# A hybrid encoder layer: the weight sums of the block products move to GpSimd, and the last 256 columns get a bank of their own

## The chip, the cores and the metric

The kernel runs on one core of a Trainium2 chip. TensorE (PE) multiplies matrices and accumulates in PSUM banks; VectorE (DVE) and ScalarE (ACT) work element by element on SBUF and PSUM; GpSimd (POOL) does so on SBUF; SyncE (SP) issues most transfers. The metric is the time of one execution on the device, in microseconds (us); less is better.

## The reference

One layer of an encoder for 512 tokens of width 1024 in float32: a pre-norm, an input projection, two token mixers in parallel (a gated linear recurrence, and a gated delta rule in chunks of 64), an output projection, then the feed-forward part, which is all that the change touches:

```python
h = rmsnorm(x, ffn_norm[l])
gu = h @ w_gate_up[l]                     # 512 x 1024 by 1024 x 5632
gt, up = jnp.split(gu, 2, axis=-1)
x = x + (jax.nn.silu(gt) * up) @ w_down[l]  # 512 x 2816 by 2816 x 1024
...
return rmsnorm(x, final_norm)
```

## The kernel before

**Splitting.** Every fp32 operand of a large matmul is split into two parts that PE takes at its faster rate: ACT copies the tile into a rounded type (`hi`), DVE subtracts to get the rest (`lo`), and three products hi·hi, hi·lo, lo·hi are accumulated. `parts_of` (L1258) does this for one tile: a copy on ACT, and a subtraction on DVE that reads two tiles in SBUF.

**Block products.** The feed-forward part cuts each product of matrices into 2 x 2 blocks and forms it from seven products in place of eight (the scheme of Strassen and Winograd). This needs sums and differences of blocks of both operands ahead of PE, and folds of the banks behind it.

- `gate_up` (L1320) makes one tile of 128 hidden columns. The first two of the 22 tiles are made plainly; the other 20 run through `gate_up`. SP loads two weight tiles `rg`, `ru` of 128 x 1024 (tag `wraw`, three buffers for all). The four sums `t1` to `t4_` (128 x 512) of their quarters b11, b12, b21, b22 are made, then all is split, and seven products of 12 matmuls of 256 columns each, 84 in all, follow. Five DVE instructions read the banks.
- The down projection contracts over 11 pairs of hidden tiles (`n2_` = 11). `down_first(j)` (L1408) uses weight block b11 and the three sums b11+b12, b12+b22 and b11+b12+b22 for four products into eight banks A, B, C, D (two each), 24 matmuls of 512 columns. DVE then folds the banks into the output `x1` and its halves. `down_second(j)` (L1432) uses the second row of blocks and one sum `t4_` for three more products, 18 matmuls; the last three j (`LASTK` = 3) are held back and end the kernel, one output block of 128 tokens after another (`last_mm`, L1516), each followed by its final norm (`finish_half`, `finish`, `write`).
- `t2_`, the sum of all three blocks, is kept in the buffers `hh` and `hl` of the normed input (`keep2`), since `down_second` needs it again; those buffers are free only when the last product of `gate_up` is done.
- `down_sums(j)` (L1114) makes two of the three sums of `down_first` in advance. It runs during the first eleven `gate_up` blocks: SP loads the blocks into `bg` and `bgb`, DVE makes two sums of 128 x 512, and SP writes them to the DRAM tile `sums`. `down_first` loads them from there.

**What sets the order.** Each helper only records its operations (class `Rec`). `Plan.order` (L148) then plays all of them through with its own costs and due times, and emits a fixed order for each engine; a due time is that of the stage (`TIMES`) plus the offset `plan.t`, and an operation can't be taken before its tiles have free buffers. So all instructions have the same line in the profile, L375, and are told apart by their tiles. In an engine's queue an instruction that waits holds up all behind it.

**At the end** the last 512 columns of token block 1 are made as twice 256 columns in the same bank of D: nine matmuls, a DVE instruction that adds the bank's first 256 columns to `x1`, nine matmuls, a DVE instruction for the second 256.

Of the kernel before, what the change touches and what calls it, by code (L numbers as in the profile page):

```python
# [26 lines left out]
NF = D_FF // P  # L27
# [20 lines left out]
N2, N4, NW = 14, 22, 3  # L48
AHEAD = 12.0
# [331 lines left out]
def trunk(ctx: ExitStack, tc: tile.TileContext, x, mix_norm, w_in, rg_conv_w, rg_conv_b, rg_wa, rg_ba, rg_wx, rg_bx,  # L381
# [3 lines left out]
    plan = Plan(nc)  # L385
    V, A, G, T = Rec(plan, "DVE", nc.vector), Rec(plan, "ACT", nc.scalar), Rec(plan, "POOL", nc.gpsimd), Rec(plan, "PE", nc.tensor)
    Q = Rec(plan, "SP", nc.sync)
# [3 lines left out]
    wp = ctx.enter_context(tc.tile_pool(name="wp", bufs=2))  # L391
# [2 lines left out]
    dn = ctx.enter_context(tc.tile_pool(name="dn", bufs=1))  # L394
    hp = ctx.enter_context(tc.tile_pool(name="hp", bufs=1))
    sp = ctx.enter_context(tc.tile_pool(name="sp", bufs=2))
    dr = ctx.enter_context(tc.tile_pool(name="dr", bufs=1, space=DRAM))
    ps = ctx.enter_context(tc.tile_pool(name="ps", bufs=3, space=PSUM))

    uid = [0]  # L400
# [5 lines left out]
    def new(pool, shape, tag, bufs, dt=F32):  # L406
        return plan.tile(pool, shape, dt, tag, bufs, nm(tag))
# [10 lines left out]
    def two(dt=F32, shape=(P, 512)):  # L418
        return new(t2, shape, "t2", N2, dt)
# [687 lines left out]
    rg_flush()  # L1107
    for n in range(KD):
        rnn_part(1, n)

    wdn = w_down[0].rearrange("(j h p) n -> p j h n", p=P, h=2)
    sums = {}

    def down_sums(j, after):  # L1114

        now = plan.t
        r, b22 = new(wp, (P, 2, 512), "bg", 2), new(wp, (P, 512), "bgb", 2)
        plan.extra = after
        Q.dma_start(r, wdn[:, j, 0, :].rearrange("p (h n) -> p h n", h=2))
        Q.dma_start(b22, wdn[:, j, 1, 512:D])  # L1120
        plan.extra = ()
        V.tensor_tensor(r[:, 0, :], r[:, 0, :], r[:, 1, :], ALU.add)
        V.tensor_tensor(r[:, 1, :], r[:, 1, :], b22, ALU.add)
        sums[j] = new(dr, (P, 2, 512), "sums", NF // 2)
        Q.dma_start(sums[j], r)
        plan.t = now

    gates = [(rnn_gate, n) for n in range(KD)] + [(dn_gate, n) for n in range(KD)]
    for g in range(4):
        spend()  # L1130
# [24 lines left out]
    for n in range(KD):  # L1155
# [1 line left out]
        y = four(F32R)  # L1157
        split(mixs[n // 2][:, n % 2, :], y)
        mh.append(y)
    last_split = (len(plan.ops) - 1,)  # L1160
    spend()


# [94 lines left out]
    def parts_of(src, hi, lo, ahead):  # L1258
        now = plan.t
        plan.t = now - ahead  # L1260
        A.copy(hi, src)
        V.tensor_tensor(lo, src, f(hi), ALU.subtract)
        plan.t = now
# [56 lines left out]
    def gate_up(n):  # L1320
        spend(10.2)
        now = plan.t
        rg, ru = new(wp, (P, 8, P), "wraw", NW), new(wp, (P, 8, P), "wraw", NW)
        plan.t = now - 40
        Q.dma_start(rg, wg[:, :, n * P:(n + 1) * P])
        Q.dma_start(ru, wg[:, :, D_FF + n * P:D_FF + (n + 1) * P])
        b11, b21, b12, b22 = rg[:, 0:4, :], rg[:, 4:8, :], ru[:, 0:4, :], ru[:, 4:8, :]
        t1, t2_, t3, t4_ = (two(shape=(P, 4, P)) for _ in range(4))
        plan.t = now - 24
        for t, x_, y_ in ((t1, b11, b12), (t2_, t1, b22), (t3, b12, b22), (t4_, t2_, b21)):  # L1330
            V.tensor_tensor(t, x_, y_, ALU.add)
        plan.t = now
        gh_, gl_ = new(wp, (P, 8, P), "whi", 2, F32R), new(wp, (P, 8, P), "wlo", 2, F32R)
        parts_of(rg, gh_, gl_, AHEAD)
        w7 = {"1": (gh_[:, 0:4, :], gl_[:, 0:4, :]), "2": (gh_[:, 4:8, :], gl_[:, 4:8, :])}
        ah, al = new(wp, (P, 8, P), "whi", 2, F32R), new(wp, (P, 8, P), "wlo", 2, F32R)
        bh, bl = four(F32R, (P, 8, P)), four(F32R, (P, 8, P))
        for i, (name, src, hi, lo) in enumerate((("6", t2_, ah, al), ("7", t3, ah, al), ("5", t1, bh, bl), ("4", t4_, bh, bl))):
            j = 4 * (i % 2)
            w7[name] = hi[:, j:j + 4, :], lo[:, j:j + 4, :]  # L1340
            parts_of(src, *w7[name], AHEAD - 1.4 * i)
        w7["3"] = two(F32R, (P, 4, P)), two(F32R, (P, 4, P))
        parts_of(b22, *w7["3"], AHEAD - 7)
# [12 lines left out]
        V.tensor_tensor(u[:, hi_], m, pc, ALU.subtract)
        product(pa, w7["2"], xs7["2"], False)
        act(s_[:, lo_], pa, AF.Silu)
        product(pd_, w7["5"], xs7["5"], True)
        V.tensor_tensor(u[:, hi_], pd_, u[:, hi_], ALU.add)  # L1360
        product(pc, w7["4"], xs7["4"], False)
        V.tensor_tensor(s_[:, hi_], pc, m, ALU.subtract)
        act(s_[:, hi_], s_[:, hi_], AF.Silu)
        product(pd_, w7["3"], xs7["3"], False)
        V.tensor_tensor(u[:, lo_], pd_, m, ALU.add)
        V.tensor_tensor(fa[n // 2][:, n % 2, :], s_, u, ALU.mult)

    for n in range(BRIDGE, NF):
        if n - BRIDGE < NF // 2:
            down_sums(n - BRIDGE, last_split)  # L1370
        gate_up(n)


# [34 lines left out]
    def down_first(j):  # L1408

        spend(5.5)  # L1410
        now = plan.t
        r1, r2 = new(wp, (P, 2, 512), "wraw", NW), new(wp, (P, 2, 512), "wraw", NW)
        hi, lo = new(wp, (P, 2, 512), "whi", 2, F32R), new(wp, (P, 2, 512), "wlo", 2, F32R)
        t2_ = keep2[j // 8][:, j % 8, :]
        plan.t = now - 40
        Q.dma_start(r2, sums[j])
        Q.dma_start(r1[:, 0, :], wdn[:, j, 0, 0:512])
        Q.dma_start(r1[:, 1, :], wdn[:, j, 1, 512:D])
        plan.t = now - 16
        V.tensor_tensor(t2_, r2[:, 0, :], r1[:, 1, :], ALU.add)  # L1420
        plan.t = now
        parts_of(r1[:, 0, :], hi[:, 0, :], lo[:, 0, :], AHEAD)
        parts_of(t2_, hi[:, 1, :], lo[:, 1, :], AHEAD)
        hi2, lo2 = four(F32R), four(F32R)
        parts_of(r2, hi2, lo2, AHEAD)
        x4 = down_q(j, True)
        w4 = [(h[:, i, :], l[:, i, :]) for h, l, i in ((hi, lo, 0), (hi, lo, 1), (hi2, lo2, 1), (hi2, lo2, 0))]
        for bank, w, x_ in zip("ABCD", w4, x4):
            for i in range(2):
                down_mm(banks[bank][i], i, w, x_, j == 0, j == n2_ - 1)  # L1430

    def down_second(j):  # L1432

        now = plan.t
        r = new(wp, (P, 2, 512), "wraw", NW)
        hi, lo = four(F32R), four(F32R)
        plan.t = now - 40
        Q.dma_start(r, wdn[:, j, 1, :].rearrange("p (h n) -> p h n", h=2))
        t4_ = two()
        plan.t = now - 16  # L1440
        V.tensor_tensor(t4_, keep2[j // 8][:, j % 8, :], r[:, 0, :], ALU.add)
        plan.t = now
        parts_of(r, hi, lo, AHEAD)
        th, tl = two(F32R), two(F32R)
        parts_of(t4_, th, tl, AHEAD)
        x3 = down_q(j, False)
        return {"2": ((hi[:, 0, :], lo[:, 0, :]), x3[2]), "3": ((hi[:, 1, :], lo[:, 1, :]), x3[0]), "4": ((th, tl), x3[1])}
# [65 lines left out]
            V.scalar_tensor_tensor(xv, xv, rin, gain3[:, n0:n0 + 256], ALU.mult, ALU.mult)  # L1513
            Q.dma_start(out[0, c * P:(c + 1) * P, n0:n0 + 256], xv)

    def last_mm(name, i, po, n0=0, n=512):  # L1516
        spend(0.7 * LASTK * n / 512)
        for w3 in last:
            (wh, wl), x_ = w3[name]
            down_mm(po[:, n0:n0 + n], i, (wh[:, n0:n0 + n], wl[:, n0:n0 + n]), x_, False, w3 is last[-1], True)  # L1520

    def weighted(c):
        xg = two()
        V.tensor_tensor(xg, x1[c][:, 0:512], gain3[:, 0:512], ALU.mult)
        return xg

    for i in range(2):
# [3 lines left out]
    for i in range(2):  # L1531
        last_mm("2", i, banks["A"][i])
        finish_half(i, 0, banks["A"][i])
        xg = weighted(i)
        if i == 0:
            last_mm("3", i, banks["D"][i])
            finish_half(i, 1, banks["D"][i])
        else:
            for n0 in (0, 256):
                last_mm("3", i, banks["D"][i], n0, 256)  # L1540
                xv = x1[i][:, 512 + n0:768 + n0]
                V.tensor_tensor(xv, banks["D"][i][:, n0:n0 + 256], xv, ALU.add)
                A.activation(two()[:, 0:256], xv, AF.Square, accum_out=ssf[:, i, 1 + n0 // 256:2 + n0 // 256])
        write(i, xg, finish(i))
    with tc.manual_schedule():
        todo = plan.order()
# [30 lines left out]
```

## Time and profile before

| | us |
|---|---|
| time, median of 3 runs | 1084.93 (1083.03 to 1085.01) |
| the profiled execution's own time | 1083.75 |
| its span in the trace | 1082.0 |
| the plain tiles and `gate_up`, on PE | up to about 963 |
| `down_first` and `down_second`, on PE | about 963 to 1064 |
| the last products and the final norm | 1064 to 1082 |

The span runs from the first to the last instruction of the trace; the rest of the time lies around it. A group of the profile names engine, operation and tiles (out<-in, without buffer numbers; many scratch tiles are just `t`), its count, busy time and mean duration. A timeline row has the start and duration in us, and in brackets how long the engine was idle before it and what ended that. `ax`, `mm` and `st` are PSUM tiles, `na` holds `x1`. Where instructions on one engine overlap, the start-to-start distance is less than the duration.

### The profile page before, as it was taken

The numbers are of one execution on the slowest core, as the hardware profiler recorded it, in microseconds if no ns is written. First come the engines' busy times: TensorE is split into PE (matmuls) and PEld (weight loads), VectorE is DVE, ScalarE is ACT, GpSimd is POOL, SyncE is SP. The second block draws the span as 40 slices with busy tenths as digits, with TensorE's granted clock in tenths as the row PEclk, the third lists the DMA queues.
The fourth block names the chain that finished last, engine by engine and source line by source line (L and its number), as shares of the span: only waits on it lengthen the run. The fifth ranks groups of instructions, "written<-read, shape, count | busy, mean of one in ns | idle before, by whom it ended". The sixth has DMA issues, their size and how long they took to land.

```text
span 1082.0 us, 17706 instructions
## 1 busy us (share of the span) xinstructions
PE 1053.9 (97%) x6793; PEld 918.9 (85%) x6793; DVE 903.2 (83%) x1631; ACT 654.8 (61%) x1182; POOL 44.2 (4%) x93
## 2 busy tenths in 40 slices
PE   6999999999999999999999999999999999999996
PEld 6988788887888888788798878689999999998885
DVE  6677999779895898689748856869999999889997
ACT  6868898887348653756566254337454454456754
POOL 2000000002020100030001000000000000000000
PEclk9999999999999999999999999999999999999998
DMA  7333323232331034103311323395475434436632
GB/s 196 97 95 100 98 64 88 83 93 73 96 90 55 25 108 116 42 20 102 93 36 45 87 75 108 109 302 159 143 228 180 128 97 114 117 101 210 196 118 96
DMA packets 165893, 118.59 MB, mean 110 GB/s; under 512 B 5681, under 2 KB 152225, under 8 KB 165809
## 3 DMA queue, kind: packets, MB, share of 16 engines
q1 hardware_dynamic: 164336, 114.18, 35.5%
q10 hardware_dynamic: 1184, 3.15, 0.8%
q8 instruction: 53, 0.87, 0.3%
q14 instruction: 32, 0.25, 0.1%
q0 software_dynamic: 288, 0.13, 0.1%
HBM read 109.59 MB, written 7.86 MB: 109 GB/s over the span
## 4 chain that ended last, share of the span: by engine, by line
PE 82%; DVE 4%; ACT 2%; issue 0%; DVEq 0%; ACTq 0%
PE mm L375 48%; PE ax L375 21%; PE st L375 13%; DVE t L375 3%; ACT na L375 1%; ACT t L375 1%; DVE na L375 1%; DVE wlo L375 0%; ACT ax L375 0%; ACT whi L375 0%; ACT L375 0%; DVEq L1572 0%; ACT drt L375 0%; DVE rin L375 0%; ACT rst L375 0%
## 5 line engine op out<-in xcount | busy, mean ns | idle before, releaser
L375 DVE TENSOR_TENSOR t<-t,t 128x512 fp32r<-128x512 f32 (+15 forms) x466 | 245.9, 540 | 14.6 <-ACT t L375 8.6
L375 PE MATMUL mm<-hh,whi 128*128 128x512 f32 (+2 forms) x704 | 242.7, 356 | 1.1 <-ACT whi L375 1.1
L375 PE MATMUL mm<-hl,whi 128*128 128x512 f32 (+2 forms) x704 | 242.2, 355 | 0.0
L375 ACT CAST whi<-wraw 128x1024 fp32r<-128x1024 f32 (+3 forms) x142 | 133.4, 940 | 152.5 <-PE mm L375 109.0
L375 DVE TENSOR_TENSOR wlo<-wraw,whi 128x1024 fp32r<-128x1024 f32 (+3 forms) x141 | 153.5, 1090 | 71.2 <-ACT whi L375 31.2
L375 PE MATMUL mm<-hh,wlo 128*128 128x512 f32 (+1 forms) x688 | 154.4, 355 | 1.1 <-DVE wlo L375 1.1
L375 PEld LDWEIGHTS mm<-hh,whi 128*128 128x128 f32 (+1 forms) x704 | 132.3, 188 | 18.8 <-ACT whi L375 1.9
L375 PEld LDWEIGHTS mm<-hl,whi 128*128 128x128 f32 (+1 forms) x704 | 132.4, 188 | 17.1 <-DVE hl L375 0.2
L375 PE MATMUL ax<-t,t 32*32 32x32 f32 (+3 forms) x1071 | 142.3, 286 | 4.0 <-DVE na L375 3.8
L375 PEld LDWEIGHTS mm<-hh,wlo 128*128 128x128 f32 x688 | 116.1, 189 | 18.6 <-DVE wlo L375 1.5
L375 PEld LDWEIGHTS ax<-t,t 128*128 128x128 f32 (+1 forms) x1071 | 111.3, 160 | 18.9 <-DVE na L375 4.0
L375 ACT CAST t<-t 128x512 fp32r<-128x512 f32 (+1 forms) x128 | 82.0, 651 | 31.5 <-DVE t L375 29.0
L375 PE MATMUL mm<-t,t 128*128 128x256 f32 (+1 forms) x468 | 91.2, 336 | 0.0
L375 PE MATMUL mm<-t,whi 128*128 128x512 f32 x320 | 82.0, 398 | 2.6 <-ACT t L375 1.8
L375 DVE SCALAR_TENSOR_TENSOR t<-mm,par,t 128x511 f32<-128x511 f32 (+1 forms) x108 | 79.9, 743 | 3.7 <-ACT t L375 2.9
L375 PEld LDWEIGHTS mm<-t,t 128*128 128x128 f32 x468 | 72.9, 190 | 8.9 <-DVE t L375 0.2
L375 ACT ACT_TABLE_LOAD x58 | 74.4, 1283 | 5.8 <-PEq L1563 1.7
L375 ACT ACTIVATE t<-t 128x128 f32<-128x128 f32 (+4 forms) x84 | 45.8, 558 | 50.3 <-DVE t L375 47.0
L375 PEld LDWEIGHTS mm<-t,whi 128*128 128x128 f32 x320 | 60.0, 190 | 17.1 <-ACT t L375 2.4
L375 ACT CAST t<-wraw 128x1024 fp32r<-128x1024 f32 (+1 forms) x48 | 41.8, 872 | 33.3 <-DMA wraw<-in_w_gate_up_dram 19.2
L375 DVE TENSOR_TENSOR t<-wraw,t 128x1024 fp32r<-128x1024 f32 (+1 forms) x48 | 47.9, 1000 | 1.3 <-ACT t L375 1.1
L375 PE MATMUL mm<-t,wlo 128*128 128x512 f32 x160 | 42.9, 395 | 0.0
(212 smaller groups left out, 1670.9 us busy)
## 6 DMA issues: line engine op xcount, KB each, us to landing
wraw<-in_w_in_dram SPq DMA_DIRECT2D x72, 512.0 KB, 3.7
wraw<-in_w_gate_up_dram SPq DMA_DIRECT2D x44, 512.0 KB, 4.0
wraw<-in_w_rnn_proj_dram SPq DMA_DIRECT2D x16, 384.0 KB, 3.5
bg<-in_w_down_dram SPq DMA_DIRECT2D x11, 512.0 KB, 5.3
sums<-bg SPq DMA_DIRECT2D x11, 512.0 KB, 3.8
wraw<-sums SPq DMA_DIRECT2D x11, 512.0 KB, 4.6
wraw<-in_w_down_dram SPq DMA_DIRECT2D x22, 256.0 KB, 2.7
wraw<-in_w_down_dram SPq DMA_DIRECT2D x11, 512.0 KB, 3.5
```

The costliest lines, as they stand in the source:

```text
L375: self.plan.add(e, lambda: real(*a, **kw), outs, ins, cost, tail, table)
```

## The change

The four sums of `gate_up` and the sum of `down_second` are made by POOL (`G`) in place of DVE (`V`). `down_sums` and the DRAM tile are gone; `down_first` loads the blocks themselves (b22 into a buffer of its own, two of them) and makes all three sums on POOL. They are asked for 24 us ahead in place of 16. Three of the four products of `x1` with the final gain move to POOL as well. At the end, the last nine matmuls of 256 columns go into a bank of B, which is free by then, and DVE adds two banks.

```diff
-    def down_sums(j, after):
...
-        Q.dma_start(r, wdn[:, j, 0, :].rearrange("p (h n) -> p h n", h=2))
-        Q.dma_start(b22, wdn[:, j, 1, 512:D])
-        plan.extra = ()
-        V.tensor_tensor(r[:, 0, :], r[:, 0, :], r[:, 1, :], ALU.add)
-        V.tensor_tensor(r[:, 1, :], r[:, 1, :], b22, ALU.add)
-        sums[j] = new(dr, (P, 2, 512), "sums", NF // 2)
-        Q.dma_start(sums[j], r)
...
         for t, x_, y_ in ((t1, b11, b12), (t2_, t1, b22), (t3, b12, b22), (t4_, t2_, b21)):
-            V.tensor_tensor(t, x_, y_, ALU.add)
+            G.tensor_tensor(t, x_, y_, ALU.add)
...
     for n in range(BRIDGE, NF):
-        if n - BRIDGE < NF // 2:
-            down_sums(n - BRIDGE, last_split)
         gate_up(n)
...
-        r1, r2 = new(wp, (P, 2, 512), "wraw", NW), new(wp, (P, 2, 512), "wraw", NW)
+        r1, r2 = new(wp, (P, 2, 512), "wraw", NW), new(wp, (P, 512), "b22", 2)
+        t13 = new(wp, (P, 2, 512), "t13", 2)
         t2_ = keep2[j // 8][:, j % 8, :]
         plan.t = now - 40
-        Q.dma_start(r2, sums[j])
-        Q.dma_start(r1[:, 0, :], wdn[:, j, 0, 0:512])
-        Q.dma_start(r1[:, 1, :], wdn[:, j, 1, 512:D])
-        plan.t = now - 16
-        V.tensor_tensor(t2_, r2[:, 0, :], r1[:, 1, :], ALU.add)
+        Q.dma_start(r1, wdn[:, j, 0, :].rearrange("p (h n) -> p h n", h=2))
+        Q.dma_start(r2, wdn[:, j, 1, 512:D])
+        plan.t = now - 24
+        G.tensor_tensor(t13[:, 0, :], r1[:, 0, :], r1[:, 1, :], ALU.add)
+        G.tensor_tensor(t13[:, 1, :], r1[:, 1, :], r2, ALU.add)
+        G.tensor_tensor(t2_, t13[:, 0, :], r2, ALU.add)
         plan.t = now
...
-        parts_of(r2, hi2, lo2, AHEAD)
+        parts_of(t13, hi2, lo2, AHEAD)
...
         t4_ = two()
-        plan.t = now - 16
-        V.tensor_tensor(t4_, keep2[j // 8][:, j % 8, :], r[:, 0, :], ALU.add)
+        plan.t = now - 24
+        G.tensor_tensor(t4_, keep2[j // 8][:, j % 8, :], r[:, 0, :], ALU.add)
...
-    def last_mm(name, i, po, n0=0, n=512):
+    def last_mm(name, i, po, n0=0, n=512, fresh=False):
...
-            down_mm(po[:, n0:n0 + n], i, (wh[:, n0:n0 + n], wl[:, n0:n0 + n]), x_, False, w3 is last[-1], True)
+            down_mm(po[:, n0:n0 + n], i, (wh[:, n0:n0 + n], wl[:, n0:n0 + n]), x_, fresh and w3 is last[0], w3 is last[-1], not fresh)
...
-        V.tensor_tensor(xg, x1[c][:, 0:512], gain3[:, 0:512], ALU.mult)
+        (G if c != 1 else V).tensor_tensor(xg, x1[c][:, 0:512], gain3[:, 0:512], ALU.mult)
...
-            for n0 in (0, 256):
-                last_mm("3", i, banks["D"][i], n0, 256)
-                xv = x1[i][:, 512 + n0:768 + n0]
-                V.tensor_tensor(xv, banks["D"][i][:, n0:n0 + 256], xv, ALU.add)
-                A.activation(two()[:, 0:256], xv, AF.Square, accum_out=ssf[:, i, 1 + n0 // 256:2 + n0 // 256])
+            last_mm("3", i, banks["D"][i], 0, 256)
+            V.tensor_tensor(xv, banks["D"][i], xv, ALU.add)
+            A.activation(two()[:, 0:256], xv[:, 0:256], AF.Square, accum_out=ssf[:, i, 1:2])
+            last_mm("3", i, banks["B"][0], 256, 256, True)
+            V.tensor_tensor(xv[:, 256:512], banks["B"][0][:, 256:512], xv[:, 256:512], ALU.add)
+            A.activation(two()[:, 0:256], xv[:, 256:512], AF.Square, accum_out=ssf[:, i, 2:3])
```

The order of instructions, first on DVE inside one `gate_up` block of before (an output of `wlo` or a `t` of `t,t` is a split; `st`, `ax` and `mm` are banks that are read):

```order
L375 TENSOR_TENSOR t_1636<-wraw_1634,wraw_1635 128x512
L375 TENSOR_TENSOR t_1638<-wraw_1635 128x512
L375 TENSOR_TENSOR t_1637<-t_1636,wraw_1635 128x512
L375 TENSOR_TENSOR t_1630<-st_1627,t_1630 128x256
L375 TENSOR_TENSOR t_1639<-t_1637,wraw_1634 128x512
L375 TENSOR_TENSOR t_1645<-t_1636,t_1644 128x512
L375 TENSOR_TENSOR t_1632<-t_1630,ax_1628 128x256
L375 TENSOR_TENSOR t_1647<-wraw_1635,t_1646 128x512
L375 TENSOR_TENSOR wlo_1641<-wraw_1634,whi_1640 128x1024
L375 TENSOR_TENSOR wlo_1643<-t_1637,whi_1642 128x512
L375 TENSOR_TENSOR wlo_1643<-t_1638,whi_1642 128x512
```

The same part of a block on DVE after the change (a `t` with `wraw` and `t` as inputs is a split too):

```order
L375 TENSOR_TENSOR t_1590<-wraw_1578,t_1589 128x512
L375 TENSOR_TENSOR t_1554<-t_1552,ax_1550 128x256
L375 TENSOR_TENSOR wlo_1563<-wraw_1556,whi_1562 128x1024
L375 TENSOR_TENSOR wlo_1565<-t_1559,whi_1564 128x512
L375 TENSOR_TENSOR wlo_1565<-t_1560,whi_1564 128x512
L375 TENSOR_TENSOR t_1554<-mm_1551,t_1554 128x256
L375 TENSOR_TENSOR t_1588<-t_1579,t_1587 128x512
L375 TENSOR_TENSOR t_1553<-ax_1550,t_1552 128x256
L375 TENSOR_TENSOR t_1588<-t_1582,t_1587 128x512
```

And POOL's rows for two such blocks after the change:

```order
L375 TENSOR_TENSOR t_1665<-wraw_1663,wraw_1664 128x512
L375 TENSOR_TENSOR t_1667<-wraw_1664 128x512
L375 TENSOR_TENSOR t_1666<-t_1665,wraw_1664 128x512
L375 TENSOR_TENSOR t_1668<-t_1666,wraw_1663 128x512
L375 TENSOR_TENSOR t_1687<-wraw_1685,wraw_1686 128x512
L375 TENSOR_TENSOR t_1689<-wraw_1686 128x512
L375 TENSOR_TENSOR t_1688<-t_1687,wraw_1686 128x512
L375 TENSOR_TENSOR t_1690<-t_1688,wraw_1685 128x512
```

The four rows that read `wraw` and no cast have left DVE's queue, which now holds splits and bank reads alone; they stand on POOL, four to a block, with nothing between.

In the down projection, DVE's rows of before for about one j (the rows that write `hh` are the kept sums; `wlo`, and `t` with two `t` inputs, are splits and differences):

```order
L375 TENSOR_TENSOR t_1784<-wraw_1780,t_1783 128x1024
L375 TENSOR_TENSOR t_1786<-t_1400,t_1785 128x512
L375 TENSOR_TENSOR hh_1742<-wraw_1780,wraw_1779 128x512
L375 TENSOR_TENSOR wlo_1782<-wraw_1779,whi_1781 128x512
L375 TENSOR_TENSOR t_1302<-t_1302 128x256
L375 TENSOR_TENSOR t_1805<-t_1498 128x512
L375 TENSOR_TENSOR wlo_1782<-hh_1742,whi_1781 128x512
L375 TENSOR_TENSOR t_1795<-t_1449,t_1794 128x512
L375 TENSOR_TENSOR t_1793<-wraw_1789,t_1792 128x1024
L375 TENSOR_TENSOR t_1795<-t_1796,t_1794 128x512
L375 TENSOR_TENSOR hh_1742<-wraw_1789,wraw_1788 128x512
L375 TENSOR_TENSOR wlo_1791<-wraw_1788,whi_1790 128x512
```

DVE's rows for about one j after the change (`t` of 128x1024 is the split of the two sums in `t13`):

```order
L375 TENSOR_TENSOR t_1512<-t_1512,t_1786 128x256
L375 TENSOR_TENSOR t_1783<-t_1781,t_1782 128x1024
L375 TENSOR_TENSOR wlo_1780<-wraw_1777,whi_1779 128x512
L375 TENSOR_TENSOR wlo_1780<-hh_1707,whi_1779 128x512
L375 TENSOR_TENSOR t_1796<-t_1555 128x512
L375 TENSOR_TENSOR t_1785<-t_1512,t_1784 128x512
L375 TENSOR_TENSOR t_1785<-t_1786,t_1784 128x512
L375 TENSOR_TENSOR t_1555<-t_1555,t_1796 128x256
L375 TENSOR_TENSOR t_1793<-t_1791,t_1792 128x1024
L375 TENSOR_TENSOR wlo_1790<-wraw_1787,whi_1789 128x512
L375 TENSOR_TENSOR wlo_1790<-hh_1707,whi_1789 128x512
```

And POOL's rows for the first four j after the change (`b` is the buffer of b22):

```order
L375 TENSOR_TENSOR t_1721<-wraw_1717 128x512
L375 TENSOR_TENSOR t_1721<-wraw_1717,b_1718 128x512
L375 TENSOR_TENSOR t_1731<-wraw_1727 128x512
L375 TENSOR_TENSOR t_1731<-wraw_1727,b_1728 128x512
L375 TENSOR_TENSOR hh_1707<-t_1721,b_1718 128x512
L375 TENSOR_TENSOR hh_1707<-t_1731,b_1728 128x512
L375 TENSOR_TENSOR t_1741<-wraw_1737 128x512
L375 TENSOR_TENSOR t_1751<-wraw_1747 128x512
L375 TENSOR_TENSOR t_1741<-wraw_1737,b_1738 128x512
L375 TENSOR_TENSOR hh_1707<-t_1741,b_1738 128x512
L375 TENSOR_TENSOR t_1751<-wraw_1747,b_1748 128x512
L375 TENSOR_TENSOR hh_1707<-t_1751,b_1748 128x512
```

The sum into `hh` has left DVE. POOL makes the sums of the first two j and then needs `hh`; from there on three sums stand in a row for each j.

Last, PE's rows where the last nine matmuls of 256 columns begin, before the change:

```order
L375 MATMUL ax_1751<-t_1936,t_1941 128x256
L375 MATMUL ax_1751<-t_1937,t_1941 128x256
L375 MATMUL ax_1751<-t_1936,t_1942 128x256
L375 MATMUL ax_1751<-t_1920,t_1925 128x256
L375 MATMUL ax_1751<-t_1921,t_1925 128x256
L375 MATMUL ax_1751<-t_1920,t_1926 128x256
```

And after it:

```order
L375 MATMUL ax_1716<-t_1912,t_1917 128x256
L375 MATMUL ax_1716<-t_1913,t_1917 128x256
L375 MATMUL ax_1716<-t_1912,t_1918 128x256
L375 MATMUL st_1711<-t_1896,t_1901 128x256
L375 MATMUL st_1711<-t_1897,t_1901 128x256
L375 MATMUL st_1711<-t_1896,t_1902 128x256
```

What followed in the same bank, `ax_1751`, now goes into `st_1711`.

More of the change, by code (lines that the diff above doesn't have):

```diff
@@ L396, in trunk @@
     sp = ctx.enter_context(tc.tile_pool(name="sp", bufs=2))
-    dr = ctx.enter_context(tc.tile_pool(name="dr", bufs=1, space=DRAM))
     ps = ctx.enter_context(tc.tile_pool(name="ps", bufs=3, space=PSUM))
@@ L1111, in trunk @@
     wdn = w_down[0].rearrange("(j h p) n -> p j h n", p=P, h=2)
-    sums = {}
-    def down_sums(j, after):
-        now = plan.t
-        r, b22 = new(wp, (P, 2, 512), "bg", 2), new(wp, (P, 512), "bgb", 2)
-        plan.extra = after
-        Q.dma_start(r, wdn[:, j, 0, :].rearrange("p (h n) -> p h n", h=2))
-        Q.dma_start(b22, wdn[:, j, 1, 512:D])
-        plan.extra = ()
-        V.tensor_tensor(r[:, 0, :], r[:, 0, :], r[:, 1, :], ALU.add)
-        V.tensor_tensor(r[:, 1, :], r[:, 1, :], b22, ALU.add)
-        sums[j] = new(dr, (P, 2, 512), "sums", NF // 2)
-        Q.dma_start(sums[j], r)
-        plan.t = now
     gates = [(rnn_gate, n) for n in range(KD)] + [(dn_gate, n) for n in range(KD)]
@@ L1159, in trunk @@
         mh.append(y)
-    last_split = (len(plan.ops) - 1,)
     spend()
@@ L1534, in trunk @@
         xg = weighted(i)
+        xv = x1[i][:, 512:D]
         if i == 0:
```

## The prediction

> **What bounds the kernel now.** I read the page's busy shares first, then the busy time of each engine by stage, then who PE waits for, then the instructions at three places.
>
> ```profile
> span 1082.0 us, 17706 instructions
> PE 1053.9 (97%) x6793; PEld 918.9 (85%) x6793; DVE 903.2 (83%) x1631; ACT 654.8 (61%) x1182; POOL 44.2 (4%) x93
> ```
>
> PE is busy 97% of the span, so taking work from another engine can win little; giving an engine too much can lose a lot. The 83% of DVE is an average, so the stages come next (columns: stretch, its length, then busy time and count of PE, PEld, DVE, ACT and POOL, PE's granted clock, DMA share, GB/s). The first two stretches hold ten `gate_up` blocks each, the third the down projection, the fourth the end.
>
> ```profile
> 760.43:860.43 100.00, 100.00 (x833) 99.81 (x833) 97.44 (x172) 47.40 (x86) 0.00 (x0) 1.00 0.55 172
> 860.43:961.18 100.75, 100.75 (x842) 100.75 (x841) 88.68 (x156) 49.61 (x90) 0.00 (x0) 1.00 0.36 105
> 963.40:1064.30 100.90, 100.90 (x458) 84.03 (x457) 99.61 (x152) 61.13 (x91) 0.00 (x0) 1.00 0.50 162
> 1064.30:1082.00 17.70, 7.63 (x37) 6.40 (x35) 10.44 (x29) 9.19 (x23) 0.00 (x0) 0.74 0.34 119
> ```
>
> PE never pauses in the first three, at full clock. A `gate_up` block takes 100.75 / 10 = 10.08 us of PE and, without sums made in advance, 88.68 / 10 = 8.87 us of DVE. In the down projection DVE is busy 99.61 of 100.90 us: PE and DVE bound this stage together, and whatever delays DVE there delays the end. POOL does nothing in any of them.
>
> **The sums move from DVE to POOL.** Three sums in a row on DVE, and the groups they belong to:
>
> ```profile
> 944.43 0.69 DVE L375 TENSOR_TENSOR t<-wraw,wraw 128x512 f32<-128x512 f32 x1
> 945.04 0.68 DVE L375 TENSOR_TENSOR t<-wraw 128x512 f32<-128x512 f32 x1
> L375 DVE TENSOR_TENSOR t<-t,wraw 128x512 f32<-128x512 f32 x20 | 13.7, 684 | 0.0
> L375 DVE TENSOR_TENSOR t<-ax,t 128x256 f32<-128x256 f32 x20 | 8.4, 421 | 5.0 <-PE ax L375 5.0
> L375 DVE TENSOR_TENSOR hh<-wraw,wraw 128x512 f32<-128x512 f32 x8 | 5.5, 686 | 0.0
> ```
>
> One lasts 0.68 us but the next starts after 0.61 us, so a sum costs DVE 0.61 us. DVE loses 4 x 20 of them in `gate_up`, 22 made in advance (already in the first stretch, under PE), and 11 + 11 in the down projection: 22 x 0.61 = 13.4 us off the stage that it bounds.
>
> POOL gains 80 + 33 + 11 sums and three products at the end. The trace shows no two-input addition on POOL, so its price is bounded by one-input rows:
>
> ```profile
> 2.08 0.28 POOL L375 TENSOR_SCALAR_AFFINE_SELECT sl<-ones 128x128 f32<-128x128 f32 x1
> 258.18 0.63 POOL L375 TENSOR_SCALAR_AFFINE_SELECT t<-t 128x512 f32<-128x512 f32 x1
> 359.01 1.41 POOL L375 TENSOR_SCALAR t<-t,dnse 128x128 f32<-128x128 f32 x4 [44.41 <-PE st L375]
> ```
>
> Going from 128 to 512 columns adds 0.35 us, 0.91 ns a column: 0.16 us fixed and 0.47 us for one read of 512. Lower end 0.63 us (the second input is free); upper end 1.41 us (four 128-column pieces at the rate of the last row). I take 0.16 + 2 x 0.47 = **1.1 us**, two inputs read one after the other, which lies between the ends. The Trainium skill (GPSIMD Engine Reference, Elementwise — side-by-side cycle accounting) gives 4497 ns for a 2048-column fp32 addition on this engine; a quarter of it, an estimate, is 1.12 us, and the sum by that would be less than 1 us longer.
>
> **The price that decides: POOL and DVE get in each other's way.** POOL has room for 1.1 us sums if they run beside DVE. Two places say that they don't; the first is three POOL operations among DVE additions with both inputs in SBUF:
>
> ```profile
> 305.35 4.54 POOL L375 TENSOR_SCALAR_AFFINE_SELECT t<-t 128x512 f32<-128x512 f32 x2 [43.71 <-ACT t L375]
> 310.08 0.63 POOL L375 TENSOR_SCALAR_AFFINE_SELECT t<-t 128x512 f32<-128x512 f32 x1 [0.20 <-ACT t L375]
> 305.77 0.41 DVE L375 TENSOR_TENSOR t<-t,t 128x238 f32<-128x238 f32 x1
> ...
> 309.31 0.83 DVE L375 TENSOR_TENSOR t<-t,t 128x234 f32<-128x234 f32 x1
> 310.82 1.22 DVE L375 TENSOR_TENSOR wlo<-wraw,whi 128x1024 fp32r<-128x1024 f32 x1 [0.68 <-issue]
> ```
>
> Two selects that need 2 x 0.63 us took 4.54 us while DVE ran one such addition after another. Then it turns round: a DVE addition of 234 columns takes 0.83 us where 238 took 0.41, and the next DVE instruction, with nothing to wait for, starts at 310.82, 0.11 us after POOL's select ends. The second place shows who is exempt:
>
> ```profile
> 569.81 5.15 POOL L375 TENSOR_SCALAR t<-t,dnse 128x128 f32<-128x128 f32 x12 [75.29 <-DVE dnse L375]
> 572.43 1.25 DVE L375 TENSOR_TENSOR wlo<-wraw,whi 128x1024 fp32r<-128x1024 f32 x1
> 371.99 2.80 POOL L375 TENSOR_SCALAR t<-t,dnse 128x128 f32<-128x128 f32 x8 [11.57 <-ACT t L375]
> 369.30 6.36 DVE L375 SCALAR_TENSOR_TENSOR na<-ax,dns,t 128x256 f32<-128x256 f32 x16 [1.05 <-PE ax L375]
> ```
>
> Twelve POOL operations at 0.35 us make 4.2 us; beside one 1.25 us DVE addition from SBUF they took 5.15. Eight took their plain 2.80 us beside sixteen DVE instructions that read one input from PSUM (`ax`). So DVE instructions with two SBUF inputs and POOL's take turns; those with a PSUM input don't. The Trainium skill (SBUF — State Buffer, Who interferes with whom) has this as a rule against the change: a DVE instruction with two SBUF inputs and a GpSimd one that reads SBUF exclude each other for the whole instruction. The trace agrees, with 4.54 us for 1.26 us of work; without the rule the sum would end at the third rival below.
>
> **The down projection.** All splits, differences and sums on DVE there read SBUF twice; only the six folds of the banks and the last block's leftovers have a PSUM input. DVE's 99.61 us less 13.4 is 86.2. POOL has 44 sums, four of which come before the stage (its order puts them ahead of the first sum that needs the `hh` buffer): 40 x 1.1 = 44.0 us in turns with DVE. About 3 us of that can lie beside the PSUM readers. 86.2 + 44.0 - 3 = 127 us against 100.9: **+26 us**. A hand-over of 0.11 us each (40 x 0.11 = 4.4) would add, and the 0.16 us fixed part of a POOL operation, if it blocks nobody (40 x 0.16 = 6.4), would take away; I let them cancel.
>
> **`gate_up`.** Per block DVE keeps 8.87 - 4 x 0.61 = 6.43 us; in turns with 4 x 1.1 = 4.4 that is 10.83 us, of which up to 5 x 0.35 = 1.75 us (the 256-column PSUM readers, 0.42 us long) may overlap: 9.1 to 10.8 against PE's 10.08. So cover is nearly gone: 0 to 0.75 us a block, 0 to 15 us over 20 blocks. I take **+5 us**. Queued behind a late sum are POOL's next sums, ACT's cast, DVE's split, and the release of one of three `wraw` buffers, so the next weight load.
>
> **The end.** PE's longest wait near the end, and the instructions around it:
>
> ```profile
> PE ax L375 <- DVE na L375: 3.8, 1, 3.8
> 1070.70 1.67 DVE L375 SCALAR_TENSOR_TENSOR na<-na,rin,t 128x256 f32<-128x256 f32 x4
> 1072.34 0.69 DVE L375 TENSOR_TENSOR t<-na,t 128x512 f32<-128x512 f32 x1
> 1072.94 0.42 DVE L375 TENSOR_TENSOR na<-ax,na 128x256 f32<-128x256 f32 x1
> 1073.42 2.29 PE L375 MATMUL ax<-t,t 128*128 128x256 f32 x9 [3.79 <-DVE na L375]
> 1075.75 0.42 DVE L375 TENSOR_TENSOR na<-ax,na 128x256 f32<-128x256 f32 x1 [1.09 <-PE ax L375]
> ```
>
> The last nine matmuls wait until DVE has read the bank's first half. With a bank of their own they run 3.8 us earlier; then DVE's queue is late, which still has the 512-wide read (0.2 us longer than now) but loses products of 0.61 us to POOL. From 1072.94 the final read could follow at about 1073.4 instead of 1075.75. **-2.5 us**, bounds -3.8 and 0.
>
> **The start and the DMAs.** The trips through DRAM vanish from SP's queue under a busy PE: nothing gained. Two 256 KB loads (`b22`) now stand in SP's order among the first weight loads:
>
> ```profile
> 9.42 7.46 SPq L375 DMA_DIRECT2D wraw<-in_w_in_dram  x3
> wraw<-in_w_down_dram SPq DMA_DIRECT2D x22, 256.0 KB, 2.7
> ```
>
> SP is held up there 7.46 us over three loads, for free buffers, and the new ones fit in that pause; I take +0.5 us, bounds 0 and 2.7 (the landing of one such load).
>
> **Sum.** 1083.75 us (the profiled execution: span 1082.0 and 1.75 around it) + 26 + 5 - 2.5 + 0.5 = 1112.75: **1113 us**. The median of the runs shown, 1084.93, is 1.2 us above the profiled one, which is small beside the unknowns.
>
> **Rivals.**
> - *The sum is cheap.* At 0.63 us POOL takes 40 x 0.63 = 25.2 us of turns: 86.2 + 25.2 - 3 = 108.4, +7.5; `gate_up` stays hidden; the end gives -2.5: about 1089. For it: one-input rows are this fast. Against: a second input must come from somewhere.
> - *DVE becomes the bound in `gate_up` too.* At 1.41 us a sum: 6.43 + 5.64 - 0.9 = 11.2 us a block, +1.1 x 20 = +22; the down stage 86.2 + 56.4 - 3 + 4.4 = 144, +43; with the start and no gain at the end: about 1151. For it: every POOL row beside SBUF additions is longer than its plain time. Against: `gate_up` has PSUM readers to overlap with.
> - *Faster: the sums run beside DVE.* If additions block each other little, DVE is relieved by 13.4 us in the down stage, PE stays the bound and only the end shows: 1083.75 - 2.5 = about 1081. It decides by what a POOL sum costs DVE: 86.2 + 40y - 3 reaches 100.9 at y = 0.44 us, and the end pays for another 0.06, so faster needs y below 0.5 us. For it: PE is the bound everywhere. Against: the two places above.
>
> **How the numbers follow.** Forecast 0.60, cheap sum 0.17, `gate_up` bound too 0.14, faster 0.09. Leaving out the last and a part of the dear case, the range is 1088 to 1148. A measurement of this kernel can tell about 0.2% (2.2 us) from no change: slower by more 0.88, within 0.04 (the cheap sum with some overlap), faster 0.08.
>
> **What would show it.** In the profile after: POOL additions 128x512 near 1.1 us where DVE is quiet and longer elsewhere; DVE additions stretched or idle with no releaser; PE waits for DVE or ACT in the down stage, which lasts about 127 us instead of 100.9; `gate_up` blocks of 10.1 to 10.8 us; no PE wait for `na` before the last nine matmuls. The forecast is wrong if PE stays unbroken through the down stage, or if a sum blocks DVE by less than 0.5 us.

## The result, and the profile after

| | before, us | after, us |
|---|---|---|
| median (lowest to highest, 4 runs each) | 1083.98 (1082.49 to 1085.01) | 1137.01 (1135.82 to 1138.25) |
| ratio, 95% interval | | 1.0494 [1.0482, 1.0507] |
| the profiled execution | 1083.75 | 1137.09 |

The change costs 53 us. The first rows of the page of after:

```profile
span 1135.3 us, 17767 instructions
PE 1071.0 (94%) x6793; PEld 925.0 (81%) x6793; DVE 910.9 (80%) x1504; ACT 651.2 (57%) x1182; POOL 270.8 (24%) x220
```

DVE has 127 instructions fewer and is not less busy (910.9 us against 903.2): those that are left have become longer. No engine is near 100% any more. To see where the time came from, both traces are cut at two places that the same PE instructions mark: the start of the last four `mm<-hh,wlo` of the first block, and the first `mm<-whi,t` of 512 columns, with which the down projection begins. The busy times by stretch, first of before, then of after (columns as ahead):

```profile
764.82:962.83 198.01, 198.01 (x1651) 197.82 (x1650) 183.37 (x325) 95.94 (x175) 0.00 (x0) 1.00 0.46 140
962.83:1082.00 119.17, 109.10 (x497) 90.91 (x495) 110.62 (x181) 70.89 (x114) 0.00 (x0) 0.96 0.47 155
```

```profile
767.89:986.25 218.36, 203.60 (x1651) 199.95 (x1650) 172.58 (x237) 94.12 (x176) 122.29 (x76) 0.99 0.32 93
986.25:1135.30 149.05, 120.68 (x497) 95.05 (x495) 129.09 (x157) 68.81 (x113) 89.71 (x43) 0.91 0.30 100
```

PE's counts are equal (1651 and 497), so the cuts are at the same work. The loss is +3.07 us up to the first mark, **+20.35** in the `gate_up` blocks and **+29.88** in the down projection with the end. In the down projection the turns can be read directly, in rows of DVE and POOL of after (start, duration):

```profile
1036.65 1.78 DVE L375 TENSOR_TENSOR wlo<-hh,whi 128x512 fp32r<-128x512 f32 x1
1037.84 1.71 POOL L375 TENSOR_TENSOR t<-wraw,b 128x512 f32<-128x512 f32 x1
1038.36 1.74 DVE L375 TENSOR_TENSOR t<-t 128x512 f32<-128x512 f32 x1
1039.51 1.71 POOL L375 TENSOR_TENSOR hl<-t,b 128x512 f32<-128x512 f32 x1
```

A DVE instruction of 0.68 us lasts 1.74 to 1.78 us here, and a sum 1.71; the next on either engine starts about 1.7 us after the last. Read as one turn each, that is 0.6 us for DVE, its plain pace, and the other 1.1 us for POOL. Where DVE is quiet, as in this row of the end (a product), a POOL operation of that form takes 1.29 us:

```profile
1118.53 1.29 POOL L375 TENSOR_TENSOR t<-na,t 128x512 f32<-128x512 f32 x1 [7.44 <-DVE na L375]
```

The `gate_up` blocks look different. DVE is busy in only 172.58 of 218.36 us there, stretched instructions included, and POOL waits. POOL's largest wait in 760 to 990 of after (us in total, times, longest):

```profile
POOL t L375 <- DMA wraw<-in_w_gate_up_dram: 67.6, 16, 6.0
```

And one pass of what repeats every 10.85 us, in rows of after (the SP row holds two loads, at 909.29 and 910.37):

```profile
904.81 1.49 POOL L375 TENSOR_TENSOR t<-wraw,wraw 128x512 f32<-128x512 f32 x1 [4.16 <-DMA wraw<-in_w_gate_up_dram]
906.26 1.29 POOL L375 TENSOR_TENSOR t<-wraw 128x512 f32<-128x512 f32 x1
907.51 3.99 POOL L375 TENSOR_TENSOR t<-t,wraw 128x512 f32<-128x512 f32 x2
908.85 1.50 DVE L375 TENSOR_TENSOR wlo<-wraw,whi 128x1024 fp32r<-128x1024 f32 x1 [0.18 <-ACT whi L375]
909.29 1.45 SPq L375 DMA_DIRECT2D wraw<-in_w_gate_up_dram  x2
915.65 1.50 POOL L375 TENSOR_TENSOR t<-wraw,wraw 128x512 f32<-128x512 f32 x1 [4.16 <-DMA wraw<-in_w_gate_up_dram]
```

The loads are issued when POOL's third sum (the first of the two at 907.51, which lasts until 909.26) and DVE's split (910.35) end. POOL's fourth sum ends at 911.50, and POOL then stands idle until the loads land. So sums, splits and loads stand one behind the other in a ring, because three `wraw` buffers hold no more than a block and a half.

**Theory**: in the down projection the turns lengthen DVE's queue, as predicted; in `gate_up` the turns alone would fit, but they stretch a ring of three buffers past PE's pace. **Rivals**: the loss comes from giving up the sums in advance; or POOL is too slow by itself; or the turns alone fill a block. The three measures in this table (differences from before, cut at the same marks in each run's trace; where nothing was changed they agree within about 1 us; the spans are rounded to 0.1) carry the experiments:

| kernel | ahead of the first mark (before: 764.82) | blocks (198.01) | down projection and end (119.17) | ratio to before, 95% |
|---|---|---|---|---|
| after | +3.07 | +20.35 | +29.88 | 1.0494 [1.0482, 1.0507] |
| e1 | +4.01 | +26.87 | +0.42 | 1.0312 [1.0293, 1.0331] |
| e2 | -0.85 | +0.01 | +28.74 | 1.0275 [1.0259, 1.0290] |
| e3 | +1.13 | -0.25 | -0.28 | 0.9995 [0.9986, 1.0004] |
| e8 | 0.00 | -0.25 | -1.25 | 0.9991 [0.9982, 1.0000] |
| e4 | +10.56 | +3.15 | +33.09 | 1.0430 [1.0414, 1.0445] |
| e12 | +2.05 | +2.73 | +32.92 | 1.0348 [1.0333, 1.0364] |
| e9 | +3.67 | +20.34 | +29.99 | 1.0487 [1.0471, 1.0503] |
| e5 | +0.35 | +0.32 | -3.87 | 0.9967 [0.9955, 0.9980] |
| e10 | -0.83 | +0.02 | +6.51 | 1.0067 [1.0052, 1.0082] |
| e6 | +3.42 | +19.22 | +7.76 | 1.0294 [1.0279, 1.0310] |
| e11 | -0.32 | -0.25 | +7.67 | 1.0059 [1.0042, 1.0075] |

### The profile page after: what moved, and what is told of

Its sections match the earlier page's. It is cut to its first block, busy times and chain, and to the rows that moved or that the text cites. A ratio compares the mean times of both kernels' runs of the same rounds, so it can differ in the third digit from the quotient of the medians.

```text
span 1135.3 us, 17767 instructions
## 1 busy us (share of the span) xinstructions
PE 1071.0 (94%) x6793; PEld 925.0 (81%) x6793; DVE 910.9 (80%) x1504; ACT 651.2 (57%) x1182; POOL 270.8 (24%) x220
## 3 DMA queue, kind: packets, MB, share of 16 engines
q10 hardware_dynamic: 1184, 3.15, 0.8%
## 5 line engine op out<-in xcount | busy, mean ns | idle before, releaser
L375 DVE TENSOR_TENSOR t<-t,t 128x512 fp32r<-128x512 f32 (+15 forms) x477 | 286.6, 615 | 29.6 <-ACT t L375 22.4
L375 DVE TENSOR_TENSOR wlo<-wraw,whi 128x1024 fp32r<-128x1024 f32 (+3 forms) x141 | 160.3, 1138 | 70.6 <-ACT whi L375 35.6
L375 ACT CAST t<-t 128x512 fp32r<-128x512 f32 (+2 forms) x139 | 92.0, 679 | 69.4 <-DVE t L375 31.6
L375 POOL TENSOR_TENSOR t<-wraw,wraw 128x512 f32<-128x512 f32 x20 | 28.8, 1442 | 256.5 <-DMA wraw<-in_w_gate_up_dram 235.9
L375 POOL TENSOR_TENSOR t<-t,wraw 128x512 f32<-128x512 f32 x40 | 74.0, 1849 | 3.9 <-DVE wlo L375 1.8
L375 POOL TENSOR_SCALAR t<-t,dnse 128x128 f32<-128x128 f32 x48 | 21.1, 459 | 224.9 <-PE ax L375 77.8
```

What stands on the lines that cost most here:

```text
L375: self.plan.add(e, lambda: real(*a, **kw), outs, ins, cost, tail, table)
```

## Experiments: one part of the change at a time

**e1**, the `gate_up` sums alone on POOL (in the kernel before):

```diff
-            V.tensor_tensor(t, x_, y_, ALU.add)
+            G.tensor_tensor(t, x_, y_, ALU.add)
```

> The kernel before, with the four sums of a gate_up block alone on GpSimd; sums in advance, down projection and end stay as they were. Theory (POOL and DVE take turns, and late sums hold the three wraw buffers): twenty blocks of about 11 us instead of 10.08 and about 3 us more at the bridge, so +20 to +26 us, 1104 to 1110 us, the down projection unchanged at about 101 us. Rival 1 (the 53 us come from giving up the sums in advance and their loads, not from GpSimd): 1084 us. Rival 2 (cover in gate_up is enough, the stage was only late because the whole is late): within 5 us of 1084.

1117.19 us: +33.5, above the theory's 20 to 26. Rivals 1 and 2 fall. That it costs more here than in after (blocks +26.87 against +20.35) goes with what else is in it: behind the first mark DVE still makes 12 of the 22 sums in advance (12 x 0.61 = 7.3 us), and their loads stand in SP's queue; the two were not separated. The other ten come ahead of the mark. In before it is eight, from 705.2 us on, so the 22 do not all lie in the first stretch of `gate_up`, as the prediction had it.

**e2**, the down projection alone: the changed kernel, with

```diff
-            G.tensor_tensor(t, x_, y_, ALU.add)
+            V.tensor_tensor(t, x_, y_, ALU.add)
```

in `gate_up`, and the end as before.

> The changed kernel with the gate_up sums on DVE again and the old end: only the down projection differs from before (its 44 sums on GpSimd, none in advance). Theory: gate_up back at 10.08 us a block, the down projection about 34 us longer than before: 1116 to 1119 us, and with the first kernel and a gain at the end of 4 us the parts add up to the 53. Rival: part of the 34 is inherited from late gate_up sums and a late queue of loads, and the stage alone costs 26 as the sum of turns had it: 1110 us.

1113.03 us, +29.3: about as far above the rival's 1110 as below the theory's 1116 to 1119. The stage itself decides for the rival: from mark to end it loses 28.74 us, nearer to 26 than to 34. Blocks and first part are as before, so the two stages' losses are separate.

**e3** and **e8**, the end alone, in the kernel before: both have

```diff
-            for n0 in (0, 256):
-                last_mm("3", i, banks["D"][i], n0, 256)
...
+            last_mm("3", i, banks["D"][i], 0, 256)
...
+            last_mm("3", i, banks["B"][0], 256, 256, True)
...
```

and e3 has the three products on POOL besides.

> The kernel before with the new end alone: bank of its own for the last 256 columns and three products on GpSimd. Theory: PE's 3.8 us wait for na is gone and the end is 4 us earlier: 1080 us. Rival (the queue of DVE was as late as the bank): 0 to 2.5 us earlier, 1081.5 to 1084.

> The kernel before with the bank of its own alone; the three products stay on DVE. If the bank makes the whole gain: 1080 us, as with the products on GpSimd. If the products on DVE are late next, as three of 0.61 us: 1081 to 1082 us. Rival: the products on GpSimd cost the end time, and this kernel is faster than the one with them by 0.5 us or more.

1083.49 and 1082.73 us: neither can be told from no change, and the 4 us of the theory aren't there. In e8 PE no longer waits for `na`, and the final read comes at 1073.66 instead of 1075.75. What is late next shows in DVE and ACT rows of e8, below a row of before:

```profile
1077.08 0.17 DVE L375 RECIPROCAL rin<-rst 128x1 f32<-128x1 f32 x1 [0.90 <-ACT rst L375]
```

```profile
1073.66 0.42 DVE L375 TENSOR_TENSOR na<-st,na 128x256 f32<-128x256 f32 x1
1074.01 0.70 ACT L375 ACTIVATE t<-t,rin 128x512 f32<-128x512 f32 x1
1074.62 0.40 ACT L375 ACTIVATE t<-na 128x256 f32<-128x256 f32 x1
1075.51 0.16 DVE L375 RECIPROCAL rin<-rst 128x1 f32<-128x1 f32 x1 [0.57 <-ACT rst L375]
```

The read ends at 1074.08, but the square of it (`t<-na`) stands behind a scaling on ACT until 1074.62; the last reciprocal is 1.57 us earlier than the 1077.08 of before, and the span 1.5. In e3, DVE waits for its turn beside POOL's products again:

```profile
1067.85 3.81 POOL L375 TENSOR_TENSOR t<-na,t 128x512 f32<-128x512 f32 x3 [491.94 <-DVE na L375]
1070.60 1.61 DVE L375 TENSOR_TENSOR t<-na,t 128x512 f32<-128x512 f32 x1
```

DVE's own product takes 1.61 us in place of 0.68. Of the kernels here that leave nothing out, e8 is the fastest, 1 us below before, and its interval reaches to no change.

## Experiments: what makes the blocks late

**e4**, four `wraw` buffers (and one `t13` buffer less, for the room):

```diff
-N2, N4, NW = 14, 22, 3
+N2, N4, NW = 14, 22, 4
...
-        t13 = new(wp, (P, 2, 512), "t13", 2)
+        t13 = new(wp, (P, 2, 512), "t13", 1)
```

> The changed kernel with four wraw buffers in place of three (t13 gives up its second buffer for the room). Theory (a loop of three buffers: POOL's stretched sums hold a block's first half, the next load waits for it, and POOL's next sums wait for that load): gate_up falls from 10.97 us a block to 10.1 to 10.3, first matmul of the down projection 12 to 18 us earlier than 986 us, whole 1120 to 1125 us. Rival (turns alone fill the block: DVE 6.43 + 4 x 1.1 us = 10.8): gate_up stays at 10.8 to 11.0 a block, whole within 3 us of 1137.

1129.73 us: 7.3 faster than after, between what the theory (12 to 17) and the rival (0 to 3) said of the whole, but the blocks answer clearly: +3.15 in place of +20.35. The busy times of the same stretch of e4:

```profile
775.38:976.54 201.16, 198.99 (x1651) 198.04 (x1649) 171.99 (x232) 94.53 (x172) 107.17 (x70) 1.00 0.34 98
```

PE is busy 198.99 of 201.16 us, with sums that still take turns; POOL's wait for loads is gone. So the turns alone fit beside PE, and it takes the ring as well to make the loss. The gain was spent elsewhere: PE reaches the first mark 10.56 us late instead of 3.07. The 3 us more in the down projection, in e12 too, may come from the `t13` buffer; that was not separated.

**e12** asks whether that is the same turns moved: e4, with the first two blocks' sums on DVE.

```diff
-            G.tensor_tensor(t, x_, y_, ALU.add)
+            (V if n < BRIDGE + 2 else G).tensor_tensor(t, x_, y_, ALU.add)
```

> The changed kernel with four wraw buffers, as in e4, and the sums of the first two gate_up blocks on DVE. In e4 the twenty blocks ran at 10.1 us, but PE lost about 7.5 us more than in the changed kernel ahead of them, where the first sums now run beside a full DVE. Theory (that loss is the same turns, moved): the last product of the first block comes at 764 to 769 us instead of 775.4, whole 1119 to 1124 us. Rival (POOL's sums had nothing to do with it: the fourth buffer's loads disturb the stage): no change, 1128 to 1131 us.

1121.54 us; the first mark falls back to 766.87. So it was POOL's sums, and not the loads of the fourth buffer: ahead of the blocks DVE has work of its own on which PE waits, and POOL's sums of the first blocks fell into it, in after as well (its 2.43 us wait of PE for `hl`, which DVE makes there). That it is their turns, and not only that POOL makes them later than DVE would, e12 doesn't tell; but in e5, below, stand-ins of the same length leave the first mark at +0.35, against +3.07 in after.

**e9** was to release a buffer one sum earlier:

```diff
-        for t, x_, y_ in ((t1, b11, b12), (t2_, t1, b22), (t3, b12, b22), (t4_, t2_, b21)):
+        for t, x_, y_ in ((t1, b11, b12), (t2_, t1, b22), (t4_, t2_, b21), (t3, b12, b22)):
```

> The changed kernel with POOL's third and fourth sum of a gate_up block exchanged, so that the block's first half (rg) is read for the last time one sum earlier; the same work on every engine. Theory of the loop: 1.1 to 1.7 us come out of the loop, blocks of 9.9 to 10.3 us, 1117 to 1127 us. Rival (turns alone): no change, 1135 to 1139 us; a third sum that comes later for its product could make it slower by up to 1 us a block.

1136.00 us, no change, but this tells nothing apart: the planner puts `t3` second in either case (in the rows above it is the `t<-wraw` at 906.26, ahead of the two `t<-t,wraw`), so every engine's order is the same as in after. It is a repetition of it, and agrees. Which reader of which buffer closes the ring stays open.

**e5**, stand-ins that wait for the same loads and take as long, but hardly read:

```diff
+    def stand_in(t, x_, y_):
+        c = 4 if len(t.shape) == 3 else 16
+        G.tensor_tensor(t[..., 0:c], x_[..., 0:c], y_[..., 0:c], ALU.add)
+        G.memset(t, 1.0)
+        G.memset(t, 1.0)
...
-            G.tensor_tensor(t, x_, y_, ALU.add)
+            stand_in(t, x_, y_)
...
```

> The changed kernel with every POOL sum of gate_up and of the down projection replaced by a stand-in: a sum of 16 columns and two memsets of 512, so that POOL waits for the same loads and is busy for about as long, but reads next to nothing from SBUF; the weight sums are left out of the result. Theory (what costs is the turns with DVE): PE is the bound again, 1080 to 1090 us. Rival (POOL is late by its own length, with or without turns): above 1115 us.

1079.97 us: faster than before. POOL's groups in 767 to 1061 of e5:

```profile
L375 POOL MEMSET t<- 128x512 f32 x210 | 105.8, 525 | 5.5
L375 POOL TENSOR_TENSOR t<-t,wraw 128x16 f32<-128x16 f32 x36 | 10.6, 295 | 1.4
```

And the busy times of e5 from the first down product to the first fold of the end:

```profile
963.50:1061.14 97.64, 97.64 (x444) 81.37 (x443) 88.43 (x133) 59.99 (x90) 58.44 (x120) 1.00 0.41 132
```

A stand-in takes 2 x 0.525 + 0.295 = 1.35 us, as long as a quiet sum, with the same three buffers, and PE never pauses. So neither POOL's own pace nor the three buffers by themselves cost anything: it takes the reading turns, and in the blocks the turns and the three buffers together. Beside stand-ins that only write, DVE's 512-column splits keep their length: 0.69 us on average, as without POOL. By the Trainium skill (SBUF — State Buffer, Who interferes with whom) a DVE instruction with two SBUF inputs contends with a GpSimd instruction that reads SBUF and not with one that only writes it; e5 agrees, with +0.32 us in the blocks. e5 also shows how little there was to win: in this kernel even sums that cost DVE nothing save only 4 us.

## Experiments: the price of a sum

**e10**, one input in place of two:

```diff
+    def stand_in(t, x_, y_):
...
+        G.affine_select(out=t, in_=x_, pattern=pat, compare_op=ALU.is_ge, fill=0.0, base=0, channel_multiplier=0)
...
-            G.tensor_tensor(t, x_, y_, ALU.add)
+            stand_in(t, x_, y_)
...
```

> The changed kernel with every POOL sum of gate_up and of the down projection replaced by a one-input operation of 512 columns (a select that passes its input through, 0.63 us where DVE is quiet); the second input is left out of the result. If one input read from SBUF takes its turn like two, for its 0.63 us or less: the down stage 86.2 + 40 x 0.63 - 3 = 108 us, gate_up hidden, 1085 to 1092 us, and the dear part of the change is the second input. Rival (it isn't the length of a turn but that POOL and DVE alternate instruction by instruction, each with a hand-over): well above that, 1100 us or more. A second rival (one input takes no turns at all): 1080 us, as with the memsets.

1091.25 us: the first case, by the sum that the cheap-sum rival had. Blocks unchanged, the down projection and end +6.51.

**e6** and **e11**, the sums of the down projection on DVE, and those of `gate_up` too in e11:

```diff
-        G.tensor_tensor(t13[:, 0, :], r1[:, 0, :], r1[:, 1, :], ALU.add)
-        G.tensor_tensor(t13[:, 1, :], r1[:, 1, :], r2, ALU.add)
-        G.tensor_tensor(t2_, t13[:, 0, :], r2, ALU.add)
+        V.tensor_tensor(t13[:, 0, :], r1[:, 0, :], r1[:, 1, :], ALU.add)
+        V.tensor_tensor(t13[:, 1, :], r1[:, 1, :], r2, ALU.add)
+        V.tensor_tensor(t2_, t13[:, 0, :], r2, ALU.add)
...
-        G.tensor_tensor(t4_, keep2[j // 8][:, j % 8, :], r[:, 0, :], ALU.add)
+        V.tensor_tensor(t4_, keep2[j // 8][:, j % 8, :], r[:, 0, :], ALU.add)
```

> The changed kernel with the down projection's sums on DVE, none in advance; gate_up and the end as changed. By DVE's own time the stage takes 99.6 + 22 x 0.61 = 113 us, against about 131 measured between its first matmul and the first fold of the end with the sums on POOL: 1137 - 16 = 1121 us. Rival (the stage is late because its loads and sums come late, not because of the turns): within 4 us of 1137.

> The changed kernel with all weight sums on DVE: what is left of the change is that no sums are made in advance, and the new end. Theory (DVE bounds the down projection by its own time): twenty blocks back at 10.08 us, the down stage 8 to 13 us longer than before, 1091 to 1096 us; so GpSimd alone costs 40 to 45 us of the 53. Rival (the loads that no longer run ahead matter as well): above 1100 us.

1115.01 us, below the expected 1121 since the stage gives back 22.1 (29.88 - 7.76) and not 16, and 1090.33 us, just under the expected 1091 to 1096. So what is left of the change in e11, giving up the sums in advance and the new end, costs 6 us (1090.33 against 1084.29), and POOL the rest, 47. The price of a sum follows from kernels that differ in nothing else of this stage. Busy times of e11, then e10, from the first down product to the end:

```profile
962.26:1089.10 126.84, 113.54 (x497) 87.84 (x495) 120.30 (x197) 69.75 (x113) 3.81 (x3) 0.98 0.36 118
```

```profile
962.02:1087.70 125.68, 110.55 (x497) 89.30 (x495) 112.20 (x157) 68.77 (x113) 51.35 (x43) 0.98 0.30 100
```

After minus e11: 149.05 - 126.84 = 22.2 us for 40 sums (DVE's counts are 157 and 197), 0.56 each above the 0.61 that a sum costs on DVE itself: **1.17 us** of the stage for a sum on POOL. e10 minus e11: -1.16 / 40 = -0.03, so **0.58 us** for one input. These are prices of the stage, DVE's waits included. The difference, 0.59, goes with the second input, about what a second read of 512 columns would take; but the one-input operation is another instruction besides.

## Why the prediction came out as it did

The sign and the mechanism held, and the time lies in the range (1088 to 1148), but 24 us above the 1113. The forecast's own bounds reach only to 1083.75 + 26 + 4.4 for hand-overs + 15 + 0 + 2.7 = 1131.9 us. That the range holds 1137 is owed to the room it left for a sum of 1.41 us, which isn't what happened: in that respect it was luck. By its terms:

- **Down projection, +26: right in size, in part by luck.** 28.74 measured in e2, and 26.91 up to the first fold of the end; a price of 1.1 us taken, 1.17 measured. But the prediction had DVE full, with 41 us of turns on top of its own 86.2. The busy times up to that fold in e2, then in after:

```profile
961.99:1091.73 129.74, 109.31 (x444) 86.66 (x443) 121.97 (x132) 59.48 (x90) 76.17 (x40) 0.92 0.30 99
```

```profile
986.25:1117.71 131.46, 110.39 (x444) 86.37 (x443) 117.97 (x133) 59.37 (x90) 85.83 (x40) 0.92 0.30 98
```

Against the 88.43 us of e5 (row above), the turns make DVE's own instructions 33.5 us longer in e2, 0.84 us a sum, and for another 7.8 us DVE is idle; in after it is 29.5 and 13.5 us. Nearly all of the idle time is DVE waiting for ACT's cast of a POOL sum that came late (7.2 us in three waits in e2, 12.5 in five in after; the last section shows one). The sum of the prediction has no such term, and its turns were too dear by about as much. The instructions with a PSUM input escaped, as it had them: in 768 to 1117 of after, the 38 of DVE's 256-column ones that lie wholly beside POOL's take 420 ns on average and 428 at most, the 62 with nothing of POOL beside them 415.

- **`gate_up`, +5, 0 to 15: the step that failed**, 20.35 measured. It weighed the turns as a sum, 9.1 to 10.8 us a block against 10.08. As to the turns this was right: with a fourth buffer PE is 99% busy in the same stretch. But engines that take turns must also have work at hand, and here POOL waited for loads that waited for the stretched sums and splits. The prediction names the loop ("the release of one of three `wraw` buffers, so the next weight load") and puts no price on it. The page of before had one, 4.0 us for a load of 512 KB to land, and a block needs two:

```profile
wraw<-in_w_gate_up_dram SPq DMA_DIRECT2D x44, 512.0 KB, 4.0
```

- **The start, +0.5.** The loads at the program's start cost nothing: at 370 us PE is 1.0 us further in after than in before. The +3.07 ahead of the first mark came at the bridge to `gate_up`, where POOL's first sums meet a DVE on which PE waits. e12 and e5 show it. The prediction had looked for turns in the stages only, not in between.
- **The end, -2.5, 0 to -3.8: too much.** 0.3 to 1.3 us where it was made alone, not to be told from none. PE's wait went, and in e8 DVE's queue puts the last read at 1073.66 (the step said 1073.4). What the step missed is ACT's queue behind it, where the square stands behind a scaling and takes back half a us; and the three products, which were to free DVE, take its turns.
- **The rivals.** "Cheap sum" (1089) had the wrong price and the right arithmetic: e10, where the price holds, gives 1091.25. "DVE becomes the bound in `gate_up` too" had about the right loss there (+22) for a wrong reason: DVE is busy in 172.58 of 218.36 us. Its parts, besides, add up to 1149, not 1151. "Faster" put its limit at about 1081 with turns of no cost: e5 gives 1079.97.

Remade with measured terms: 1083.75 + 28.7 + 20.4 + 3.1, and +1.1 in after's last stretch over e2's, is 1137.1. As all but the 28.7 are stretches of after's own trace, that they add up proves nothing; what each stretch is made of rests on the separate kernels.

## What to carry to other kernels

Before moving work to an idle engine, ask whether the two take turns at something: look for rows in which an instruction of either engine has about the summed length of both, before adding up busy times. Then ask what each lengthened instruction holds: a step that fits by throughput can still lengthen a ring of buffer, load and reader past the pace of the engine that bounds the stage, and here either another buffer (e4 with e12) or a shorter turn (e10) repaired it. A gain that vanishes in one stage is looked for in the next (e4), with marks at the same instructions of both traces.

## What was not expected of the hardware

- **The turns aren't always fair.** Three of after's 40 sums in the down projection lasted 7.04, 9.57 and 8.27 us, while DVE ran its instructions back to back at their plain lengths. The last of them, three of DVE's rows beside it, and what came of it:

```profile
1088.74 8.27 POOL L375 TENSOR_TENSOR t<-hh,wraw 128x512 f32<-128x512 f32 x1 [5.52 <-DMA wraw<-in_w_down_dram]
...
1089.36 0.94 DVE L375 TENSOR_TENSOR t<-t,t 128x768 fp32r<-128x768 f32 x1
1090.23 0.67 DVE L375 TENSOR_TENSOR na<-na,t 128x512 f32<-128x512 f32 x1
1090.84 1.21 DVE L375 TENSOR_TENSOR t<-wraw,t 128x1024 fp32r<-128x1024 f32 x1
...
1097.04 1.36 ACT L375 CAST t<-t 128x512 fp32r<-128x512 f32 x2 [4.28 <-POOL t L375]
1097.69 3.08 DVE L375 TENSOR_TENSOR t<-t,t 128x512 fp32r<-128x512 f32 x2 [1.84 <-ACT t L375]
```

DVE has nothing ready from 1095.85 on, the sum ends at 1097.01, ACT casts it, and only then DVE goes on. So what POOL loses in this way comes back later as idle time of DVE. When the two alternate and when they don't, the runs don't show.

- **PE is slower behind a wait.** After a wait of 3.35 us, 512-column matmuls of after follow each other at 0.43 us instead of 0.23, for some 3.5 us (1021.1 to 1024.6), and again from 1031.0 to 1034.4 after one of 1.97 us:

```profile
1021.10 1.22 PE L375 MATMUL mm<-whi,t 128*128 128x512 f32 x2 [3.35 <-DVE t L375]
1022.12 0.63 PE L375 MATMUL mm<-wlo,t 128*128 128x512 f32 x1
1022.54 0.63 PE L375 MATMUL mm<-whi,t 128*128 128x512 f32 x1
...
1024.60 0.40 PE L375 MATMUL st<-wlo,t 128*128 128x512 f32 x1
1024.83 0.39 PE L375 MATMUL st<-whi,t 128*128 128x512 f32 x1
```

The same 497 matmuls are busy 120.68 us in after and 109.10 before, at a granted clock of 0.91 against 0.96. Whether that lengthened the stage, beside DVE's queue, was not tried.
